# Two-layer mixer encoder, 512 x 1024, on one core: six places of the written order of ScalarE and VectorE and the place of the gates' bias rows

## The chip, the core and the metric

The kernel runs on one core of a Trainium2 chip. A core has five engines that work side by side: TensorE (PE, matrix products into the PSUM banks), VectorE (DVE), ScalarE (ACT), GpSimd (POOL) and SyncE (SP). In this kernel SP and POOL only issue transfers. PEld in the profile is PE loading stationary operands. The metric is the device time of one execution in microseconds, as the median of several; less is better.

## The reference, cut to what matters

```python
for l in range(2):                       # x: 512 tokens x 1024 channels, float32
    x = x + 0.5 * swiglu(rms_norm(x, ...), ffn1_w_in[l], ffn1_w_out[l])
    x = x + mixer(rms_norm(x, ...), ...)
    x = x + 0.5 * swiglu(rms_norm(x, ...), ffn2_w_in[l], ffn2_w_out[l])
return rms_norm(x, final_norm)

def mixer(h, ...):
    z = h @ w_in                         # columns: q, k, v (512 each), uf (512), ga, gf (1024 each)
    y_na = neighbourhood_attention(q, k, v, rpb) @ w_na_out   # 8 heads of 64
    y_f = fourier_mix(uf) @ w_f_out      # real part of a 2-D DFT per group of 128 channels
    g_na = sigmoid(ga + gate_bias[0])
    g_f = sigmoid(gf + gate_bias[1])
    return (g_na * y_na + g_f * y_f) @ w_o
```

A token attends to a window of 8 rows by 16 columns of its 8 x 64 grid, with a learned bias per head.

## The kernel before, in words

**Precision and splits.** Products are done in float32r: each operand is split into a high half (a copy that ACT rounds, `S.activation(hi, t, AF.Copy)`) and a low half (DVE, `t - hi`), and three products are summed (high by high, high by low, low by high; `mm3`, lines 293 to 295, and `late_low`, 469 to 472). So each new operand costs ACT one copy and DVE one subtraction before PE can use it. Weights are split in the same way: a `Stream` takes them in one fixed list, eight are fetched ahead into `raw` tiles (line 147), and `prep` makes `whi` on ACT (line 178) and `wlo` on DVE (line 181). There are three buffers each for `whi` and `wlo`. `ws.prep(ws.pos + n)` prepares weights until n are ready beyond the position of PE; `ws.next(ahead)` takes one and prepares `ahead` more.

**Seven products.** Products of two by two blocks (u with v, the gates, the output) take seven products of sums (Strassen's scheme), named m1 to m7, with combined activations t4 to t7 (`combos`) and three pairs of PSUM banks A, B, C that are snapshot (`snap`, line 539) or subtracted (`less`, line 544).

**The mixer's first part** (`proj_UV` and the block behind it): u and v together in seven parts, with the projections q0, k0, q1, k1 of the first head pairs between them (`proj_T`: 24 matmuls of 512 columns, 8 of the channel tiles by 3). Then come k's and q's of the other pairs, the DFT (`four_pos`, `rotated`, `four_ch`, `four_q`, `four_y`, `four_high`), the scores of head pairs 0 and 1 (`att_scores`, line 1212), their softmax (`Probs`: `maxes` on DVE, `exps` on ACT, `inverse` on DVE, `scaled` on ACT, line 1245), the transposes of the probabilities (line 1264) and the products with v (`att_pv`). v has four blocks of 128 rows, each with `v_high` on ACT (line 1046) and `v_low` on DVE (line 1049). `vs` are three more blocks, shifted by half a block: six copies from one part of the local memory to another, issued by SP (lines 1486 and 1487).

**What sets the order.** In this part the order of ACT, DVE and PE is written by hand (`tc.manual_schedule`): each engine runs its instructions in the order of the program text. The transfers are not in that list; they are placed by the scheduler and run in order on SP and POOL. Tiles come from pools with a fixed number of buffers: 23 of 4 KB per partition under the tag `k` (`slot`, `hilo`; weights, splits, snapshots and bias rows share them), 11 `tmp`, four `bm` (attention bias), 8 PSUM banks. An instruction whose tile takes over a buffer waits for that buffer's last reader.

**The gates** follow: rows of n (`fill(o, ns, 0, w)`: the attention's output times its matrix), then two gate blocks in the order m1, m5, m2, m6, m7, m3, m4, whose weights are partly sums made by accumulating transfers on POOL (lines 149 and 183). Two bias rows of 1024 (`gb`, line 1606) are fetched to all partitions and read at line 1350.

Of the kernel before, what the change touches and what calls it, by code (L numbers as in the profile page):

```python
# [9 lines left out]
F32 = mybir.dt.float32  # L10
F32R = mybir.dt.float32r
# [6 lines left out]
P = 128  # L18
# [71 lines left out]
def encoder_kernel(  # L90
# [19 lines left out]
    def slot(dt=F32, s="k", shape=(4, 256)):  # L110
        return kp.tile([P, *shape], dt, tag="k", name=nm(s), bufs=23)
# [864 lines left out]
    def stage_mixer(l, norm, nxt):  # L976
# [25 lines left out]
        def proj_T(scale, ahead=AHEAD, hook=None):  # L1002
            ps = bank()
            wh, wl = ws.next(ahead)
            for kt in range(DT):
                if hook and kt == 5:
                    hook()
                c = slice(kt * P, (kt + 1) * P)
                mm3(ps, wh[:, c], wl[:, c], *xs[kt], kt == 0, kt == DT - 1)

            def out():
                t = tmp(s="q")
                V.tensor_tensor(t, ps, R, ALU.mult)
                hi, lo = hilo("q")
                if scale is None:
                    S.activation(hi, t, AF.Copy)
                else:
                    S.activation(hi, t, AF.Copy, scale=scale)

                def rest():  # L1020
                    if scale is None:
                        V.tensor_tensor(lo, t, hi.bitcast(F32), ALU.subtract)
                    else:
                        V.scalar_tensor_tensor(lo, t, scale, hi.bitcast(F32), ALU.mult, ALU.subtract)
                    return hi, lo

                return rest

            return out

        def high_of(t, s):

            hi, lo = hilo(s)
            S.activation(hi, t, AF.Copy)

            def low_of():
                V.tensor_tensor(lo, t, hi.bitcast(F32), ALU.subtract)
                return hi, lo

            return low_of  # L1040
# [3 lines left out]
        def v_high(b, src):  # L1044
            vt[b] = slot(F32R, "v", (2, T))
            S.activation(vt[b][:, 0, :], src, AF.Copy, scale=norm.r[:, b : b + 1])

        def v_low(b, src):
            V.scalar_tensor_tensor(
                vt[b][:, 1, :], src, norm.r[:, b : b + 1], vt[b][:, 0, :].bitcast(F32), ALU.mult, ALU.subtract  # L1050
            )

        def proj_UV():

            acts, combine = combos(norm, None)
            ws.depth = 8
            steps = {m: combine(m) for m in (5, 6, 7, 4)}

# [12 lines left out]
            next(root)  # L1071
            ws.items[ws.prepped + 1].summed()
            next(root)
            norm.spread(R)
            ws.prep(ws.pos + 3)
            low10 = norm.quad_high(*norm.due.pop(0))
            s1 = snap(pa)
            norm.low01()
            step(6, 2)
            pb = pair("B")  # L1080
            product(pb, acts[5], K4, True, hook=low10)
            sb = snap(pb)
            S.activation(small("sq", 1), ones, AF.Exp)
            step(6)
            q0 = proj_T(DH**-0.5)
            step(7, 2)
            product(pa, acts[6], K4, False, again=True, hook=lambda: step(7))
            s2 = snap(pa)
            k0 = proj_T(None)
            step(4, 2)  # L1090
            q0 = q0()
            step(4)
            pc = pair("C")
            product(pc, acts[2], K4, True)
# [24 lines left out]


            k1 = proj_T(None, hook=turn)
            constants()
            us, ue = [[], []], []
            for c in range(2):
                for op in (ALU.add, ALU.subtract):
                    w = tmp(s="ue")
                    V.scalar_tensor_tensor(w, s1[:, c, :], norm.r[:, c : c + 1], flipped[c], ALU.mult, op)
                    ue.append(high_of(w, "u"))
                    us[c].append(None)
            for i, low_of in enumerate(ue):  # L1130
# [315 lines left out]
        with tc.manual_schedule(engines={mybir.EngineType.DVE, mybir.EngineType.Activation}):  # L1446
            with tc.manual_schedule(engines={mybir.EngineType.PE}):
# [7 lines left out]
                bt.append(rotated(fp[1]))  # L1455
                bh.append(high_of(bt[1], "b"))
                less(pa, sb)
                for c in range(2):
                    v_high(2 + c, sb[:, c, :])
                k[1] = k1()  # L1460
                b_ = [bh[0](), bh[1]()]
                q2 = proj_T(DH**-0.5)
# [1 line left out]
                p0, p1 = [Probs(i, att_scores(i)) for i in range(2)]  # L1464
                p0.maxes(0)
                p0.maxes(1)
                p0.exps(0)
                p1.maxes(0)
                p0.inverse(0)
# [2 lines left out]
                p0.inverse(1)  # L1472
                p1.exps(0)
                product(pa, acts4, K4, False, again=True, ahead=0)
                ws.prep(ws.pos + 1)
                q[2] = q2()
                for c in range(2):
                    v_high(c, pa[c])
                f0, f1 = four_ch(b_[0]), four_ch(b_[1])
                g0, g1 = four_q(f0[1]), four_q(f1[1])  # L1480
                for c in range(4):
                    v_low(c, sb[:, c - 2, :] if c > 1 else pa[c])
                vs = []
                for s in range(3):
                    t = slot(F32R, "vs", (2, T))
                    nc.sync.dma_start(out=t[0:64].bitcast(F32), in_=vt[s][64:128].bitcast(F32))
                    nc.sync.dma_start(out=t[64:128].bitcast(F32), in_=vt[s + 1][0:64].bitcast(F32))
                    vs.append(t)
                bias_for(1)
                p1.exps(1)  # L1490
                fp = [four_pos(2), four_pos(3)]
# [1 line left out]
                p1.inverse(0)  # L1493
                y1 = four_y(f1[0], g1)
                p1.inverse(1)
                ws.prep(ws.pos + 2)
                k2 = proj_T(None, 1)
                y0 = four_high(y0)
                y1 = four_high(y1)
                p0.scaled(0)  # L1500
                p0.scaled(1)
                bt = [rotated(fp[0])]
                bh = [high_of(bt[0], "b")]
                p1.scaled(0)
                bt.append(rotated(fp[1]))
                bh.append(high_of(bt[1], "b"))
                p1.scaled(1)
                b_ = [bh[0](), bh[1]()]
                k2 = k2()
                ws.prep(ws.pos + 2)  # L1510
                fq = []

                def second():
# [4 lines left out]
                g0, g1 = four_q(f0[1]), four_q(f1[1])  # L1518
                w0 = four_y(f0[0], g0)
                w1 = four_y(f1[0], g1)  # L1520
                w0 = four_high(w0)
                w1 = four_high(w1)
                yf += [y0(), y1()]
                q3 = q3()
                ts = transposed(p0.s) + transposed(p1.s)
                ph = [high_of(t, "p") for t in ts]
                ph = [h() for h in ph]
                pt_ = {0: ph[0:2], 1: ph[2:4]}
                p2, p3 = [Probs(i, att_scores(i)) for i in (2, 3)]
# [69 lines left out]
        att_outs(3)  # L1599
        t12, _ = next(first)  # L1600
        ws.prep(ws.pos + 2)
        bias = []
        for which in range(2):
            b_ = slot(F32, "gb", (D,))
            src = bass.AP(tensor=gbias.tensor, offset=gbias.offset + (2 * l + which) * D, ap=[[0, P], [1, D]])
            nc.sync.dma_start(out=b_, in_=src)
            bias.append(b_)
        acts = {1: (hx[0], lx[0], 0), 2: (hx[1], lx[1], 0), 3: (hx[1], lx[1], 256), 4: (hx[0], lx[0], 256)}

        def high(src, s):  # L1610
# [20 lines left out]
            w = [ws.next(), ws.next()]  # L1631
        for _ in fill(o, ns, 0, w):
            pass

        def behind_weights():
            return tc.issue_after(ws.items[ws.prepped - 1].last.ins)
# [253 lines left out]
```

## Time and profile before

| | us |
|---|---|
| median of 3 runs | 1923.67 (1921.34 to 1924.65) |
| the profiled execution, its device time | 1926.9 |
| its span, first to last instruction | 1923.7 |
| PE busy / DVE / ACT / POOL | 1894.6 / 1639.2 / 1193.4 / 171.5 |
| granted clock of PE, mean | 0.995 |

The span has six stages: FFN, mixer, FFN, and the same again. Times in the text are from the span's start. The first layer's mixer begins near 335 us and its gates near 500; the second layer's mixer begins near 1290.

How to read a line of the timeline: start, duration, engine, line of the code, operation, written tile <- read tiles, shapes, count; in brackets, how long the engine stood idle before it, and what ended that. `x2` means that two instructions in a row are put together. A matmul line has the time to the end of its result, while the next one starts earlier: a 512-column matmul shows 0.39 us and starts every 0.227 us at full clock.

### The profile page before, as it was taken

How to read it: one execution, taken by the hardware profiler on the slowest of the kernel's cores; microseconds unless marked ns; L12 is line 12 of the kernel's file. 1: busy time of each engine (PE TensorE's matmuls, PEld its weight loads, DVE VectorE, ACT ScalarE, POOL GpSimd, SP SyncE). 2: the span in 40 equal slices, each digit the busy share in tenths (PEclk: the TensorE clock that was granted, in tenths of full speed). 3: DMA queues.
4: the chain of work that ended last, by engine and by line, in shares of the span. 5: the costliest groups of instructions: out<-in, count | busy, mean ns of one | idle time of the engine just before them, and what ended most of it. 6: DMA issues, size and time to landing. Idle time of an engine off the chain costs nothing.

```text
span 1923.7 us, 25086 instructions
## 1 busy us (share of the span) xinstructions
PE 1894.6 (98%) x9149; PEld 1583.0 (82%) x9149; DVE 1639.2 (85%) x1992; ACT 1193.4 (62%) x1714; POOL 171.5 (9%) x210
## 2 busy tenths in 40 slices
PE   9999999999999999999999999999999999999998
PEld 7888888887788888888888888888788878888886
DVE  8878899776889987789998878998769889777899
ACT  6655666658555855566665556666685567555664
POOL 0100010100111010101010100101001101010010
PEclk9999999999999999999999999999999999999999
DMA  9776498931986777749877765988229867776594
GB/s 298 204 212 176 153 257 262 215 98 50 258 200 174 168 202 208 185 149 256 254 178 218 183 175 168 273 261 179 83 91 264 214 159 173 210 182 176 169 274 142
DMA packets 106939, 372.74 MB, mean 194 GB/s; under 512 B 12288, under 2 KB 12416, under 8 KB 106816
## 3 DMA queue, kind: packets, MB, share of 16 engines
q1 hardware_dynamic: 78144, 272.80, 42.2%
q0 software_dynamic: 28528, 98.33, 28.2%
q8 instruction: 71, 1.16, 0.2%
q14 instruction: 52, 0.43, 0.1%
q10 hardware_dynamic: 144, 0.02, 0.0%
HBM read 365.85 MB, written 2.11 MB: 191 GB/s over the span
## 4 chain that ended last, share of the span: by engine, by line
PE 80%; DVE 7%; DMA 5%; issue 4%; ACT 4%; POOL 0%; SPq 0%; DVEq 0%; ACTq 0%; POOLq 0%
PE A L469 9%; PE A L470 9%; PE A L472 9%; PE o L472 6%; PE o L470 6%; PE o L469 5%; PE B L469 5%; PE B L470 5%; PE B L472 5%; DMA raw<-in_wst_dram 4%; PE C L470 2%; PE C L469 2%; PE C L472 2%; DVE wlo L181 2%; PE ps L295 2%
## 5 line engine op out<-in xcount | busy, mean ns | idle before, releaser
L181 DVE TENSOR_TENSOR wlo<-raw,whi 128x1024 fp32r<-128x1024 f32 (+1 forms) x536 | 638.0, 1197 | 185.5 <-ACT whi L178 184.4
L178 ACT ACTIVATE whi<-raw 128x1024 fp32r<-128x1024 f32 (+1 forms) x536 | 553.1, 1037 | 387.7 <-PE A L470 127.8
L149 POOL DMA_DIRECT2D raw<-in_wst_dram x166 | 144.4, 896 | 1412.8 <-DMA raw<-in_wst_dram 740.8
L163 DVE TENSOR_TENSOR raw<-raw,raw 128x1024 f32<-128x1024 f32 (+1 forms) x150 | 178.1, 1196 | 1.2
L470 PE MATMUL A<-whi,xl 128*128 128x512 f32 x400 | 155.7, 389 | 0.0
L469 PE MATMUL A<-whi,xh 128*128 128x512 f32 x400 | 155.7, 389 | 0.0
L472 PE MATMUL A<-wlo,xh 128*128 128x512 f32 x400 | 115.1, 389 | 0.0
L174 DVE SCALAR_TENSOR_TENSOR wlo<-raw,whi 128x1024 fp32r<-128x1024 f32 (+1 forms) x83 | 98.1, 1198 | 15.8 <-ACT whi L173 15.8
L173 ACT ACTIVATE whi<-raw 128x1024 fp32r<-128x1024 f32 (+1 forms) x83 | 85.8, 1036 | 40.6 <-PE o L470 12.8
L674 ACT ACTIVATE th<-sn,rh 128x512 f32<-128x512 f32 x80 | 56.8, 714 | 70.7 <-DVE sn L544 70.7
L539 ACT ACTIVATE sn<-A 128x512 f32<-128x512 f32 x104 | 60.7, 589 | 46.5 <-PE A L472 46.3
L472 PEld LDWEIGHTS A<-wlo,xh 128*128 128x128 f32 x400 | 74.9, 188 | 15.8 <-DVE wlo L174 0.3
L470 PEld LDWEIGHTS A<-whi,xl 128*128 128x128 f32 x400 | 75.1, 188 | 15.4
L469 PEld LDWEIGHTS A<-whi,xh 128*128 128x128 f32 x400 | 75.1, 188 | 15.4
L469 PE MATMUL C<-whi,xh 128*128 128x512 f32 x208 | 81.1, 390 | 0.0
L470 PE MATMUL C<-whi,xl 128*128 128x512 f32 x208 | 81.0, 389 | 0.0
L470 PE MATMUL B<-whi,xl 128*128 128x512 f32 x208 | 81.0, 389 | 0.0
L469 PE MATMUL B<-whi,xh 128*128 128x512 f32 x208 | 80.9, 389 | 0.0
L472 PE MATMUL C<-wlo,xh 128*128 128x512 f32 x208 | 59.8, 389 | 0.0
L472 PE MATMUL B<-wlo,xh 128*128 128x512 f32 x208 | 59.8, 389 | 0.0
L293 PE MATMUL ps<-xh,whi 128*128 128x512 f32 x128 | 52.3, 409 | 4.3 <-ACT fq L1168 2.5
L469 PE MATMUL B<-whi,t5h 128*128 128x512 f32 x136 | 54.2, 399 | 0.0
(447 smaller groups left out, 4798.7 us busy)
## 6 DMA issues: line engine op xcount, KB each, us to landing
raw<-in_wst_dram SPq DMA_DIRECT2D x470, 512.0 KB, 5.3
raw<-in_wst_dram POOLq DMA_DIRECT2D x174, 512.0 KB, 8.0
raw<-in_wst_dram SPq DMA_DIRECT2D x30, 256.0 KB, 4.2
bm<-in_bias_dram SPq DMA_DIRECT2D x16, 384.0 KB, 3.7
vs<-v SPq DMA_DIRECT2D x12, 256.0 KB, 4.6
x<-in_xin_dram SPq DMA_DIRECT2D x4, 512.0 KB, 10.2
raw<-in_wst_dram POOLq DMA_DIRECT2D x8, 256.0 KB, 9.1
dft<-in_dft_dram POOLq DMA_DIRECT2D x8, 256.0 KB, 4.2
```

Of the source, the lines that this page charges most:

```text
L149: G.dma_start(out=self.t, in_=wst[GRAN_AT[self.plus]][:, 0 : self.n], accum_op=ALU.add)
L163: V.tensor_tensor(self.raw.t, self.raw.t, self.add.t, ALU.add)
L173: S.activation(hi, t, AF.Copy, scale=-1.0)
L174: self.last = V.scalar_tensor_tensor(lo, t, -1.0, hi.bitcast(F32), ALU.mult, ALU.subtract)
L178: S.activation(hi[:, cs], t[:, cs], AF.Copy)
L181: self.last = V.tensor_tensor(lo[:, cs], t[:, cs], hi[:, cs].bitcast(F32), ALU.subtract)
L293: PE.matmul(ps, lh, rh, start=start, stop=False, skip_group_check=again)
L469: PE.matmul(ps, lh, rh, start=start, stop=False, skip_group_check=again)
L470: PE.matmul(ps, ll, rh, start=False, stop=False, skip_group_check=again)
L472: PE.matmul(ps, lh, rl, start=False, stop=stop, skip_group_check=again)
L539: S.activation(t[:, b, :], ps[b], AF.Copy)
L674: S.activation(th[:, b, :], g[:, b, :], AF.Tanh, scale=norm.rh[:, c : c + 1])
```

## The change

Six places of the written order are changed, and the bias rows' fetch. No instruction is added or left out, and no PE order changes.

1. In `proj_UV`, t7 is made in three steps at three places instead of two: the subtraction behind q0's product, the high half in the hook of m6's product, the low half behind k0's product.
2. The high halves of v's rows 2 and 3 go from behind `less(pa, sb)` to behind k2's product; the weight of k2 is prepared ahead of p0's exponentials instead of behind m4's product.
3. The low halves of v's rows 2 and 3, and the copies `vs`, go behind the preparation of k3's weight.
4. q3's weight is prepared behind the first `rotated` (after the high halves of y), not ahead of k2's product.
5. `scaled` of p0 and p1 and the high halves of b are interleaved in another order.
6. q3's evacuation is cut in two: t (DVE) ahead of the high halves of w and the low halves of y, the high half (ACT) behind the high halves of the transposed probabilities.
7. The two bias rows are fetched behind the rows of n.

```diff
-            def out():
+            def out(now=True):
...
-                if scale is None:
-                    S.activation(hi, t, AF.Copy)
-                else:
-                    S.activation(hi, t, AF.Copy, scale=scale)
+                def high():
+                    if scale is None:
+                        S.activation(hi, t, AF.Copy)
+                    else:
+                        S.activation(hi, t, AF.Copy, scale=scale)
+                    return rest
...
-                return rest
+                return high() if now else high
...
             q0 = proj_T(DH**-0.5)
-            step(7, 2)
+            step(7)
             product(pa, acts[6], K4, False, again=True, hook=lambda: step(7))
             s2 = snap(pa)
             k0 = proj_T(None)
+            step(7)
             step(4, 2)
...
                 less(pa, sb)
-                for c in range(2):
-                    v_high(2 + c, sb[:, c, :])
                 k[1] = k1()
...
                 p0.maxes(0)
                 p0.maxes(1)
+                ws.prep(ws.pos + 3)
                 p0.exps(0)
...
                 product(pa, acts4, K4, False, again=True, ahead=0)
-                ws.prep(ws.pos + 1)
                 q[2] = q2()
...
-                for c in range(4):
-                    v_low(c, sb[:, c - 2, :] if c > 1 else pa[c])
-                vs = []
...
+                for c in range(2):
+                    v_low(c, pa[c])
                 bias_for(1)
...
                 p1.inverse(1)
-                ws.prep(ws.pos + 2)
-                k2 = proj_T(None, 1)
+                k2 = proj_T(None, 0)
+                for c in range(2):
+                    v_high(2 + c, sb[:, c, :])
                 y0 = four_high(y0)
                 y1 = four_high(y1)
+                bt = [rotated(fp[0])]
+                ws.prep(ws.pos + 1)
                 p0.scaled(0)
+                bh = [high_of(bt[0], "b")]
                 p0.scaled(1)
-                bt = [rotated(fp[0])]
-                bh = [high_of(bt[0], "b")]
-                p1.scaled(0)
                 bt.append(rotated(fp[1]))
                 bh.append(high_of(bt[1], "b"))
+                p1.scaled(0)
                 p1.scaled(1)
                 b_ = [bh[0](), bh[1]()]
                 k2 = k2()
                 ws.prep(ws.pos + 2)
+                for c in range(2):
+                    v_low(2 + c, sb[:, c, :])
+                vs = []
...
                 fq = []
...
                 w1 = four_y(f1[0], g1)
+                q3 = q3(False)
                 w0 = four_high(w0)
                 w1 = four_high(w1)
                 yf += [y0(), y1()]
-                q3 = q3()
                 ts = transposed(p0.s) + transposed(p1.s)
                 ph = [high_of(t, "p") for t in ts]
+                q3 = q3()
                 ph = [h() for h in ph]
...
         ws.prep(ws.pos + 2)
-        bias = []
-        for which in range(2):
-            b_ = slot(F32, "gb", (D,))
...
         for _ in fill(o, ns, 0, w):
             pass
+        bias = []
+        for which in range(2):
+            b_ = slot(F32, "gb", (D,))
...
```

More of the change, by code (lines that the diff above doesn't have):

```diff
@@ L1480, in stage_mixer @@
                 g0, g1 = four_q(f0[1]), four_q(f1[1])
-                for c in range(4):
-                    v_low(c, sb[:, c - 2, :] if c > 1 else pa[c])
-                vs = []
[L1484 to L1488, printed above, removed]
+                for c in range(2):
+                    v_low(c, pa[c])
                 bias_for(1)
@@ L1510, in stage_mixer @@
                 ws.prep(ws.pos + 2)
+                for c in range(2):
+                    v_low(2 + c, sb[:, c, :])
+                vs = []
+                for s in range(3):
+                    t = slot(F32R, "vs", (2, T))
+                    nc.sync.dma_start(out=t[0:64].bitcast(F32), in_=vt[s][64:128].bitcast(F32))
+                    nc.sync.dma_start(out=t[64:128].bitcast(F32), in_=vt[s + 1][0:64].bitcast(F32))
+                    vs.append(t)
                 fq = []
@@ L1601, in stage_mixer @@
         ws.prep(ws.pos + 2)
-        bias = []
-        for which in range(2):
-            b_ = slot(F32, "gb", (D,))
-            src = bass.AP(tensor=gbias.tensor, offset=gbias.offset + (2 * l + which) * D, ap=[[0, P], [1, D]])
-            nc.sync.dma_start(out=b_, in_=src)
-            bias.append(b_)
         acts = {1: (hx[0], lx[0], 0), 2: (hx[1], lx[1], 0), 3: (hx[1], lx[1], 256), 4: (hx[0], lx[0], 256)}
@@ L1633, in stage_mixer @@
             pass
+        bias = []
+        for which in range(2):
+            b_ = slot(F32, "gb", (D,))
+            src = bass.AP(tensor=gbias.tensor, offset=gbias.offset + (2 * l + which) * D, ap=[[0, P], [1, D]])
+            nc.sync.dma_start(out=b_, in_=src)
+            bias.append(b_)
         def behind_weights():
```

## The prediction

> **What bounds the kernel now.** I read the page first: TensorE (PE) is busy for all but 29 us of the span, so a changed order can win only idle PE time and time at a lowered clock.
>
> ```profile
> span 1923.7 us, 25086 instructions
> PE 1894.6 (98%) x9149; PEld 1583.0 (82%) x9149; DVE 1639.2 (85%) x1992; ACT 1193.4 (62%) x1714; POOL 171.5 (9%) x210
> ```
>
> Then PE's waits between 320 and 480 us, which is the first layer's mixer up to its attention (the columns: total, times, longest):
>
> ```profile
> PE ps L293 <- ACT fq L1168: 1.3, 1, 1.3
> PE ps L1212 <- DVE q L1013: 1.2, 1, 1.2
> PE ps L294 <- DVE b L1037: 1.1, 1, 1.1
> PE ps L293 <- DVE p L1037: 1.0, 1, 1.0
> ```
>
> All are waits for ACT or DVE; the second layer has the same four. So in this stretch the two engines' common chain, not PE, sets the end, while the stretches behind it have almost no PE idle (windows; first the length, then PE busy, later DVE busy):
>
> ```profile
> 404.20:437.60 33.40, 28.77 (x173) 24.15 (x170) 24.89 (x64) 23.07 (x50) 0.00 (x0) 0.99 0.33 88
> 416.50:421.50 5.00, 5.00 (x23) 4.13 (x22) 5.00 (x13) 3.17 (x9) 0.00 (x0) 1.00 0.66 158
> 455.00:484.00 29.00, 29.00 (x184) 25.43 (x183) 16.99 (x55) 25.60 (x73) 0.00 (x0) 1.00 0.16 55
> 560.00:1280.00 720.00, 719.88 (x3465) 605.07 (x3464) 629.69 (x670) 442.41 (x571) 66.25 (x78) 1.00 0.74 203
> ```
>
> So whatever PE gains by 455 us stays. From 404.2 to 437.6 DVE is busy for 24.89 of 33.40 us: 8.5 us idle. DVE's rows show the ends of that stretch (end of the b lows, first maximum of p2) and the waits:
>
> ```profile
> 402.91 1.29 DVE L1037 TENSOR_TENSOR b<-bt,b 128x512 fp32r<-128x512 f32 x2
> ...
> 406.96 1.23 DVE L181 TENSOR_TENSOR wlo<-raw,whi 128x1024 fp32r<-128x1024 f32 x1 [2.76 <-ACT whi L178]
> ...
> 414.51 1.23 DVE L181 TENSOR_TENSOR wlo<-raw,whi 128x1024 fp32r<-128x1024 f32 x1 [1.77 <-ACT whi L178]
> ...
> 429.34 1.23 DVE L181 TENSOR_TENSOR wlo<-raw,whi 128x1024 fp32r<-128x1024 f32 x1 [1.65 <-ACT whi L178]
> ...
> 435.20 2.48 DVE L1037 TENSOR_TENSOR p<-ps,p 128x512 fp32r<-128x512 f32 x4 [1.18 <-ACT p L1034]
> ...
> 437.60 0.42 DVE L1228 CUSTOM_DVE_ANT_0 s<-ps,bm 128x256 f32<-128x256 f32 x1
> ```
>
> ACT's rows show where the first two come from:
>
> ```profile
> 404.64 1.34 ACT L1046 ACTIVATE v<-sn,r 128x512 fp32r<-128x512 f32 x2 [2.72 <-PE ps L1212]
> ...
> 409.94 0.63 ACT L1018 ACTIVATE q<-q 128x512 fp32r<-128x512 f32 x1 [3.01 <-PE A L470]
> ...
> 414.38 1.24 ACT L1046 ACTIVATE v<-A,r 128x512 fp32r<-128x512 f32 x2
> 415.52 0.63 ACT L1168 ACTIVATE fq<-ps 128x255 f32<-128x255 f32 x2
> ...
> 419.82 1.36 ACT L1182 ACTIVATE y<-fy 128x512 fp32r<-128x512 f32 x2 [1.73 <-DVE fy L1175]
> ```
>
> The high halves of v's rows 2 and 3 need only `sb`, yet they wait 2.72 us for the first scores: their buffers are, I take it, those of q0 and k0, which these scores read last. Behind them stand m4's second weight and then q2's high half, which waits another 3.01 us for a product that it doesn't read: a full buffer pool again.
>
> **The change, part by part.** No arithmetic is added. The same DVE instructions lie between the b lows and p2's first maximum, so p2 moves by what becomes of the 8.5 us idle.
>
> *v's high halves 2 and 3 go behind k2's product, k2's weight ahead of p0's exponentials.* ACT is free at 404.64 - 2.72 = 401.9, makes m4's weight by 403, and DVE its low half at 404.2: the wait of 2.76 goes. q2's product then gives t at 405.4 and its high half at 406.1 to 406.7, now in q0's buffer, released at 404.6. k2's weight follows to 407.7 while DVE does p0's maxima until 407.4: a wait of 0.35 in place of 1.77. Next late are v's highs 0 and 1: ACT ends its three exponential pairs at 410.5 (2.9 us, as between the high half of 409.94 and the weight that DVE splits at 414.51) and PE its product at about 410.2, so DVE waits 0.3 near 411.2. The reads of pa and fq now end by 412.6, so k2's product finds its bank at 414.5: the PE wait of 1.3 goes.
>
> *q3's weight and the order of rotated and scaled.* From 410.5 ACT does two v highs (1.24), two fq (0.63), an exponential pair (about 1), two more v highs (1.34), two y highs (1.36), and then q3's weight (1.04), ready at 417. DVE ends its first rotated at 416.1 and waits 0.85: a new wait, with the second rotated and both b lows queued behind it. They end at 421.6 instead of 427.0; PE asks for b at 423.4 (414.5, plus 39 matmuls at 5.00/22 = 0.227 us, from the window row). The 1.1 goes. The scaled of p0 and p1 end near 422.4, ahead of the transposes at 427.
>
> *v's low halves 2 and 3 behind k3's weight.* The wait for that weight's high half stays, 1.65 plus 0.15 for ACT's scaled ahead of it. The two lows stood ahead of the b lows; they now stand ahead of the w rows: neutral on DVE. The moved weight steps issue no loads: eight weights are fetched ahead, and this stage's are out by then. POOL's queue is not touched.
>
> *q3's t ahead of the y lows, its high half behind the p highs.* The bank is free at 428.7, before PE asks, and ACT can start the p highs earlier: the waits of 1.18 (DVE) and 1.2 and 1.0 (PE) go.
>
> Left of DVE's idle: 0.35 + 0.3 + 0.85 + 0.15 + 1.8 = 3.4 us. So p2's maxima come 8.5 - 3.4 = **5.1 us** earlier. From there to p3's scaled the order is unchanged, and the chain arrives 5.1 us earlier there too. PE gets there sooner still: k3 at 430.7, 24 matmuls to 436.1, 36 shorter and longer ones to about 442, and the first eight transposes to 443. Its last transposes wait for p3's scaled:
>
> ```profile
> 449.72 1.71 ACT L1245 ACTIVATE s<-s,rs 128x256 f32<-128x256 f32 x4
> ...
> 451.08 0.87 PE L1264 MATMUL ps<-ident,s 128*128 128x128 f32 x6 [0.36 <-ACT s L1245]
> ```
>
> ACT is there at 444.6 now, so the hole of 0.8 us (0.4 and 0.4) becomes one of about 3 (2.4 and 0.6). That is the new bound of the stretch, and the gain is the chain's 5.1, not PE's 6. The second layer also has a wait of 0.45 of its own now, which put its maxima 0.3 later; its gain is 5.4:
>
> ```profile
> 1384.93 0.42 DVE L1173 TENSOR_TENSOR fy<-ps,fq 128x256 f32<-128x256 f32 x1 [0.45 <-DVE fq L1167]
> ```
>
> *The hole and the clock.* Windows of 3.41 us at the borders where the granted clock changes (eighth number):
>
> ```profile
> 412.72:416.13 3.41, 2.13 (x18) 1.93 (x17) 1.64 (x3) 3.41 (x10) 0.00 (x0) 1.00 0.54 181
> 433.20:436.61 3.41, 1.54 (x14) 1.28 (x15) 2.23 (x5) 2.55 (x6) 0.00 (x0) 1.00 0.00 0
> 436.61:440.02 3.41, 3.41 (x10) 2.65 (x9) 3.41 (x11) 2.92 (x10) 0.00 (x0) 0.50 0.02 5
> 525.36:528.77 3.41, 3.41 (x9) 2.65 (x8) 3.41 (x3) 1.90 (x2) 0.56 (x1) 0.50 1.02 303
> 1385.52:1388.93 3.41, 1.99 (x26) 1.64 (x24) 2.75 (x7) 1.89 (x4) 0.00 (x0) 1.00 0.01 2
> ```
>
> A window in which PE was busy for 1.54 or 1.99 us is followed by half clock, one with 2.13 isn't. Three idle microseconds within 3.3 leave at least one window under 2.0 however the borders fall. Half a window, **1.7 us**, is lost behind the hole, in the part that PE bounds. (Today's two slow stretches lie ahead of the chain's end and cost nothing.) If the second window is caught too it is 3.4; bounds 0 and 3.4. The Trainium skill's page "TensorE: Matmul & The Clock Gate", section "Why this matters for your kernels", speaks against this loss: it asks for no idle gap above some 3 us, one idle window bringing half clock. By that rule no clock would be lost; the rows here show half clock behind windows that were 45 and 58% busy.
>
> *t7 in three places, around k0.* ACT made t7's high half, waiting for DVE, ahead of k0's weight. Now the weight goes first, and a PE wait of 0.5 goes:
>
> ```profile
> 360.93 0.50 PE L295 MATMUL ps<-xh,wlo 128*128 128x512 f32 x1 [0.48 <-DVE wlo L181]
> ```
>
> t7's product starts some 28 us later; its lateness is hidden. If that cover were gone, the cost would be one split, 1.2 us.
>
> *The copies `vs` on SP.* Four of the six now follow the v lows that end at 426.5.
>
> ```profile
> 417.08 0.53 SPq L1486 DMA_DIRECT2D vs<-v  x1
> ...
> 420.83 1.10 SPq L1487 DMA_DIRECT2D vs<-v  x1
> ...
> 440.91 1.08 SPq L1197 DMA_DIRECT2D bm<-in_bias_dram  x2
> ...
> DMA to landing us min/median/max: 3.1/4.6/5.2
> ```
>
> Six issues take 4.85 us now; four from 426 land by 434.5 at the latest, and the first product that reads one starts at 436.1. Hidden, with some 2 us to spare.
>
> *The bias rows on SP.* They are issued behind c's first weight instead of ahead of it:
>
> ```profile
> 484.30 1.01 SPq L1606 DMA_DIRECT2D gb<-in_gbias_dram x2
> ...
> 516.56 0.75 DVE L1350 SCALAR_TENSOR_TENSOR sn<-sn,r,gb 128x512 f32<-128x512 f32 x1
> ...
> 522.77 1.06 ACT L178 ACTIVATE whi<-raw 128x1024 fp32r<-128x1024 f32 x1 [2.43 <-DMA raw<-in_wst_dram]
> ...
> 524.36 0.50 PE L469 MATMUL A<-whi,t3h 128*128 128x512 f32 x1 [1.94 <-ACT sn L539]
> ...
> DMA to landing us min/median/max: 9.1/10.8/12.3
> ...
> PE A L469 <- ACT sn L539: 0.8, 1, 0.8
> ```
>
> Their first reader runs 32 us after the issue, and they land within 12.3 (the bias rows' own view): a few microseconds later is free. The last row is the same place in the second layer. The PE wait of 1.94 here hangs on an accumulated weight that starts only after its tile was split; I take no change, between 0 and the whole wait.
>
> Sum: first layer 5.1 + 0.5 - 1.7 = 3.9, second 5.4 + 0.5 - 1.7 = 4.2: **8.1 us**. The profiled execution took 1926.9, its span 1923.7; the median of the runs is 1923.67, and I take the 8.1 from that: **1915.6**.
>
> **Rivals.** *The clock holds*: the hole costs no window; 3.4 more, 1912.2. For it: two windows with the wait at 414 passed. Against: three idle microseconds are more than any of them had. It is what the Trainium skill's rule above would give.
>
> *The gates' hole closes*: without the bias rows ahead, the accumulated weights come early enough; 1.94, its slow window (525.36) of 1.7 and the second layer's 0.8 go: 4.4 more, 1911.2. Against: that weight waits for a DVE split, not for the queue.
>
> *The buffer pool stays full* (the change doesn't do what it says): q2's high half still waits until 409.9. Then k2's low half starts at 411.3, DVE waits 3.6 us more, and 5.1 shrinks to 1.6, which the clock eats: 1.3 left, 1922.4. For it: the pool's order is not in the profile.
>
> *Slower: the copies come too late.* If SP gives them out behind the next pair's bias rows (440.91, 435.3 after), the last is issued at 441.2 and lands at 446.4. PE needs it from 436 on; half of that product, the rows of f and the transposes then end at 452.4, against 451.95 now, and the hole of 10 us costs at least a slow window, 1.7: 2.2 per layer, 1928. It decides once a copy lands some 10 us after its place in the sum.
>
> **How the numbers follow.** Forecast 0.45, clock holds 0.13, gates' hole closes 0.12, pool stays full 0.18, copies too late 0.12. This kernel's measurement can tell about 0.2%, 3.85 us, from no change: the first three are faster (0.70), the fourth the same (0.18), the fifth slower (0.12). The range reaches from both faster rivals nearly together, 1908, to the pool's case, 1923; beyond it lie the copies.
>
> **What would show it.** Right: ACT's q2 row no longer waits for A; no PE waits for fq, b or q3; p2's maxima 5 us sooner; a PE wait of 2 to 3 us at L1264 for s, with a half-clock window behind it. Wrong: q2 still waiting near 410 for PE; PE waiting at L293 to L295 for vs; L1350 waiting for gb.

## The result and the profile after

The changed kernel takes **1907.09 us** (median of 4 runs, 1904.92 to 1907.68), the kernel before 1923.45 (4 runs beside it, 1921.34 to 1924.65): a ratio of 0.9914, 95% interval 0.9897 to 0.9931, or 16.4 us less. The prediction said 8.1 less, and at the lowest 1908. So the direction was right and the size wrong by half.

The section on the change says that no PE order changes. That holds for the order written by hand. Outside it the program's scheduler also moved something when the bias rows were moved: two neighbouring products in the rows of n changed places on PE, and on ACT the high half of t1 came forward. The second of these gave a late transfer 1.2 us more room, as the experiments show.

The page and PE's waits over the whole span, after:

```profile
span 1902.9 us, 25094 instructions
PE 1885.3 (99%) x9149; PEld 1580.2 (83%) x9149; DVE 1639.2 (86%) x1992; ACT 1194.7 (63%) x1714; POOL 171.5 (9%) x210
```

```profile
PE ps L1269 <- ACT s L1250: 4.8, 4, 2.0
...
PE A L469 <- ACT sn L539: 0.4, 1, 0.4
```

The waits for fq, b, q, p and for k0's weight are gone, and the hole for p3's scaled has come where the prediction put it (line 1264 before is line 1269 now). But the gates' wait (A for sn) has shrunk from 2.8 us to 0.4, which the prediction had left standing.

To see where the time came from, one reads the start of the same matmul in both traces. These are, twice (once for each layer), the first matmul of k0, of m2's product C behind it, of the rows of n, and of the gates' product B. Before:

```profile
359.84 0.39 PE L293 MATMUL ps<-xh,whi 128*128 128x512 f32 x1
366.09 0.39 PE L469 MATMUL C<-whi,xh 128*128 128x512 f32 x1
487.66 0.39 PE L293 MATMUL ps<-whi,o 128*128 128x512 f32 x1
530.20 0.39 PE L469 MATMUL B<-whi,xh 128*128 128x512 f32 x1
...
1313.79 0.39 PE L293 MATMUL ps<-xh,whi 128*128 128x512 f32 x1
1320.01 0.39 PE L469 MATMUL C<-whi,xh 128*128 128x512 f32 x1
1441.92 0.39 PE L293 MATMUL ps<-whi,o 128*128 128x512 f32 x1
1481.73 0.39 PE L469 MATMUL B<-whi,xh 128*128 128x512 f32 x1
```

After:

```profile
358.85 0.39 PE L293 MATMUL ps<-xh,whi 128*128 128x512 f32 x1
364.29 0.39 PE L469 MATMUL C<-whi,xh 128*128 128x512 f32 x1
480.70 0.39 PE L293 MATMUL ps<-whi,o 128*128 128x512 f32 x1
519.43 0.39 PE L469 MATMUL B<-whi,xh 128*128 128x512 f32 x1
...
1302.88 0.39 PE L293 MATMUL ps<-xh,whi 128*128 128x512 f32 x1
1308.32 0.39 PE L469 MATMUL C<-whi,xh 128*128 128x512 f32 x1
1424.14 0.39 PE L293 MATMUL ps<-whi,o 128*128 128x512 f32 x1
1463.46 0.39 PE L469 MATMUL B<-whi,xh 128*128 128x512 f32 x1
```

The differences between neighbouring rows give the length of each stretch:

| stretch | layer 1: before, after, gain | layer 2: before, after, gain | forecast gain |
|---|---|---|---|
| k0 | 6.25, 5.44, **0.81** | 6.22, 5.44, **0.78** | 0.5 + 0.5 |
| mixer and attention | 121.57, 116.41, **5.16** | 121.91, 115.82, **6.09** | 3.4 + 3.7 |
| gates | 42.54, 38.73, **3.81** | 39.81, 39.32, **0.49** | 0 |

That is 17.1 us. The two profiled spans differ by 20.8; the other 3.7 us lie where the change touches nothing (0.99 of it ahead of k0: 359.84 against 358.85). Such stretches vary from execution to execution; the execution profiled before was 3.2 above its median, the one after 2.2 below.

In the gates' first layer, 1.9 of the 3.81 is PE's wait, and most of the rest is the half-clock window that stood behind it (525.36 in the prediction). The window doesn't always come: in e1, a kernel described below, the second layer has a wait of 1.95 and the window and takes 42.55, the first has a wait of 1.57 and no window and takes 40.53.

In the mixer's chain, the same rows as the prediction showed, after:

```profile
401.11 1.28 DVE L1041 TENSOR_TENSOR b<-bt,b 128x512 fp32r<-128x512 f32 x2
...
404.23 0.63 ACT L1021 ACTIVATE q<-q 128x512 fp32r<-128x512 f32 x1 [3.16 <-DVE q L1014]
...
405.84 1.22 DVE L181 TENSOR_TENSOR wlo<-raw,whi 128x1024 fp32r<-128x1024 f32 x1 [0.34 <-ACT whi L178]
...
421.73 1.23 DVE L181 TENSOR_TENSOR wlo<-raw,whi 128x1024 fp32r<-128x1024 f32 x1 [1.78 <-ACT whi L178]
...
430.06 0.42 DVE L1233 CUSTOM_DVE_ANT_0 s<-ps,bm 128x256 f32<-128x256 f32 x1
```

ACT's q2 no longer waits for PE's A but for DVE's own q. From b's low halves to p2's first maximum DVE takes 28.95 us (430.06 - 401.11), where it took 34.69 (437.60 - 402.91): 5.74 less. In the second layer it is 6.07 less (28.96 against 35.03). The prediction had 5.1 and 5.4.

The hole and what ran behind it, first layer and second. First the windows of the granted clock (eighth number), then PE's rows:

```profile
440.37:443.78 3.41, 1.03 (x8) 0.56 (x7) 2.49 (x4) 2.76 (x7) 0.00 (x0) 1.00 0.47 156
443.78:447.19 3.41, 3.41 (x28) 3.08 (x28) 2.29 (x6) 2.43 (x7) 0.00 (x0) 0.50 0.00 0
1382.44:1385.86 3.42, 2.31 (x15) 1.79 (x13) 3.33 (x7) 1.58 (x4) 0.00 (x0) 1.00 0.15 35
1385.86:1389.27 3.41, 2.14 (x20) 1.62 (x20) 1.83 (x4) 3.36 (x8) 0.00 (x0) 1.00 0.30 119
```

```profile
442.74 0.44 PE L1269 MATMUL ps<-ident,s 128*128 128x128 f32 x2 [2.02 <-ACT s L1250]
443.54 1.35 PE L1269 MATMUL ps<-ident,s 128*128 128x128 f32 x6 [0.36 <-ACT s L1250]
444.82 2.74 PE L1217 MATMUL ps<-q,q 64*128 64x256 f32 x24
447.49 0.50 PE L293 MATMUL ps<-whi,y 128*128 128x512 f32 x1
...
1386.77 0.44 PE L1269 MATMUL ps<-ident,s 128*128 128x128 f32 x2 [2.01 <-ACT s L1250]
1387.56 0.88 PE L1269 MATMUL ps<-ident,s 128*128 128x128 f32 x6 [0.36 <-ACT s L1250]
1388.37 1.32 PE L1217 MATMUL ps<-q,q 64*128 64x256 f32 x13
1389.91 0.97 PE L1217 MATMUL ps<-q,q 64*128 64x256 f32 x11 [0.21 <-DVE p L1041]
1390.91 0.50 PE L293 MATMUL ps<-whi,y 128*128 128x512 f32 x1
```

The two holes are alike (2.02 and 2.01, then 0.36). In the first layer one window holds nearly all of it, PE is busy for 1.03 us in it, and half clock follows. In the second the border of two windows cuts the hole, 2.31 and 2.14 are left, and the clock holds. From the hole's end to the rows of y the first layer takes 4.75 us and the second 4.14: the half-clock window cost 0.6, not 1.7. The second layer's 4.14 holds a wait of 0.21 for p that the first doesn't have, so by estimate the slower matmuls alone cost some 0.8.

### The profile page after: what moved, and what is told of

Its sections match the earlier page's. It is cut to its first block, busy times and chain, and to the rows that moved or that the text cites. A ratio compares the mean times of both kernels' runs of the same rounds, so it can differ in the third digit from the quotient of the medians.

```text
span 1902.9 us, 25094 instructions
## 1 busy us (share of the span) xinstructions
PE 1885.3 (99%) x9149; PEld 1580.2 (83%) x9149; DVE 1639.2 (86%) x1992; ACT 1194.7 (63%) x1714; POOL 171.5 (9%) x210
## 4 chain that ended last, share of the span: by engine, by line
PE 89%; DVE 5%; ACT 3%; issue 2%; DMA 1%; DVEq 0%; POOL 0%; ACTq 0%; POOLq 0%
PE A L469 10%; PE A L470 10%; PE A L472 10%; PE o L470 7%; PE o L469 7%; PE o L472 7%; PE B L469 5%; PE B L470 5%; PE B L472 5%; PE C L469 2%; PE C L470 2%; PE C L472 2%; PE tr L592 2%; PE ps L293 2%; PE ps L294 2%; PE ps L295 2%
## 5 line engine op out<-in xcount | busy, mean ns | idle before, releaser
L694 DVE TENSOR_TENSOR at<-at,at 128x1024 f32<-128x1024 f32 (+1 forms) x48 | 53.8, 1130 | 0.0
```

The costliest lines, as they stand in the source:

```text
L694: V.tensor_tensor(dst, in0, in1, op)
```

## The experiments

Theories at the start. **A**: the bias rows' move closed the gates' hole. **C** (the prediction's): the rows' place is worth nothing. For the mixer: the prediction's reasons, place by place, with their sizes open. Twelve runs follow, one of them the changed kernel again (e9), in three groups; the kernel before, run beside each group, had medians of 1923.01, 1922.59 and 1922.97.

### The gates

**e1**, the changed kernel with the rows' fetch back at its old place; **e2**, the kernel before with the rows' move alone:

```diff
         ws.prep(ws.pos + 2)
+        bias = []
+        for which in range(2):
...
+            bias.append(b_)
         acts = {1: (hx[0], lx[0], 0), 2: (hx[1], lx[1], 0), 3: (hx[1], lx[1], 256), 4: (hx[0], lx[0], 256)}
...
         for _ in fill(o, ns, 0, w):
             pass
-        bias = []
-        for which in range(2):
...
-            bias.append(b_)
```

(This is e1; e2 makes the opposite move in the kernel before.)

> The changed kernel with the bias rows' fetch alone at its old place, ahead of the rows of n; all else as changed. On SP the two issues stand ahead of three weight loads again, and on ACT the high half of t1 stands again behind the four splits of o instead of ahead of them. Theory A (the bias rows' move closed the gates' hole, 3.8 us in the first layer and 0.4 in the second): 1911.3, 4.2 above the changed kernel, with PE's wait of about 2 us at the gates' last product of A back in the first layer. Theory C (the prediction: the rows' place is worth nothing; the hole closed because the mixer delivers earlier): 1907.1, no such wait.

> The kernel before with the bias rows' move alone. Theory A: the gates' hole closes here too: 4.2 to 4.4 us off, 1919.2, and PE does not wait for ACT's sn at the gates. Theory C: 1923.4, and the wait of 1.9 us stays, since the mixer is as late as before.

e1: 1909.0 (ratio to before 0.9929, 0.9915 to 0.9942), 1.9 above the changed kernel, with gate waits of 1.6 and 1.9 us in its profile (of an execution of 1912.4). e2: 1919.75 (0.9985, 0.9976 to 0.9994), 3.3 below before, with waits of 0.2 and 0.5. e1's interval overlaps the changed kernel's, so its 1.9 isn't certain by itself; e2's lies below 1. So C falls by e2: moving the rows is worth some 3 us by itself, 1.2 to 4.6 by the interval.

**e3** asks in which way. The rows stay late, t1's high half is tied behind the last split of o:

```diff
-            S.activation(hi, src, AF.Copy)
+            split.last = S.activation(hi, src, AF.Copy)
...
-            h1 = high(t12, "t1")
+            with tc.issue_after(split.last.ins):
+                h1 = high(t12, "t1")
```

> The changed kernel with the bias rows at their new place, but the high half of t1 on ACT tied behind the last split of o, where it stood before the change. It parts two ways in which the rows' move can act. Theory A1 (order: t1's high half goes ahead on ACT, so m1's weight and all of DVE's work at the gates run 1.2 us earlier): PE waits again for some 0.7 to 2 us in the first layer, and with its half-clock window the time is 1909 to 1911. Theory A2 (transfer: two rows read by all partitions stand ahead of the weights on the queue, and the weights land later): nothing changes, 1907.1.

1907.92 (1906.78 to 1913.3; ratio 0.9927, 0.9912 to 0.9941): by the median, between the two theories and nearer to A2. But three runs lie at 1906.8 to 1907.9 and two at 1912.4 and 1913.3, and the profile is of the 1912.4. The tie also let some of ACT's snapshots and weights at the gates change their order, so t1 isn't all that e3 moves. The traces say more. In the timeline of before, ACT, DVE and POOL at the gates, and the weight that PE waits for:

```profile
491.03 1.06 ACT L1612 ACTIVATE t1h<-t 128x1024 fp32r<-128x1024 f32 x1
492.00 1.04 ACT L173 ACTIVATE whi<-raw 128x1024 fp32r<-128x1024 f32 x1
493.07 1.22 DVE L174 SCALAR_TENSOR_TENSOR wlo<-raw,whi 128x1024 fp32r<-128x1024 f32 x1 [1.61 <-ACT whi L173]
...
514.80 0.85 POOL L183 DMA_DIRECT2D raw<-in_wst_dram  x1 [11.72 <-DVE wlo L181]
```

After:

```profile
480.16 1.06 ACT L1614 ACTIVATE t1h<-t 128x1024 fp32r<-128x1024 f32 x1 [0.33 <-DVE t L1594]
...
484.26 1.21 DVE L174 SCALAR_TENSOR_TENSOR wlo<-raw,whi 128x1024 fp32r<-128x1024 f32 x1
...
506.55 0.85 POOL L183 DMA_DIRECT2D raw<-in_wst_dram  x1 [15.58 <-DVE wlo L181]
...
513.62 1.06 ACT L178 ACTIVATE whi<-raw 128x1024 fp32r<-128x1024 f32 x1 [0.31 <-PE A L470]
```

And e3, first and second layer:

```profile
509.11 0.86 POOL L183 DMA_DIRECT2D raw<-in_wst_dram  x1 [15.30 <-DVE wlo L181]
...
514.99 1.06 ACT L178 ACTIVATE whi<-raw 128x1024 fp32r<-128x1024 f32 x1 [0.32 <-PE A L470]
...
1453.58 0.85 POOL L183 DMA_DIRECT2D raw<-in_wst_dram  x1 [16.41 <-DVE wlo L181]
...
1461.76 1.06 ACT L178 ACTIVATE whi<-raw 128x1024 fp32r<-128x1024 f32 x1 [2.66 <-DMA raw<-in_wst_dram]
```

Before, t1's high half comes on ACT behind the splits of o, m1's weight behind it, and DVE waits 1.61 us; everything that DVE does at the gates hangs on that, up to the split which releases the accumulation of line 183. After, t1 is ahead of three of the splits and DVE doesn't wait. Against the first matmul of t2's product, the accumulation is issued 1.9 us early in the kernels with t1 forward (1.88 to 1.93 in all 20 stretches of ten traces) and 0.7 early in those with t1 late (0.65 to 0.69 in 8 of 8, e3 among them). PE needs the sum about 5.2 us after that matmul. In e3's first layer ACT split the sum 5.9 us after the issue (509.11 to 514.99; it waited last for PE, not for the transfer, and PE then didn't wait), in the second 8.2 after it (1453.58 to 1461.76: PE waits 2.2). So two things are shown: the order of t1 gives the transfer 1.2 us more room, and the landing varies by over 2 us, so that a single execution may show a wait of 2 us or none.

The landing times in all fourteen traces bear this out. The transfer landed 5.5 to 8.1 us after its issue, and PE's wait is what goes beyond 5.9 us where t1 is late (8 stretches; 7.86 and a wait of 1.94 in the first layer of before) and beyond 7.1 where it is forward (20 stretches; 7.56 and 0.42 in the second layer of after), to within 0.1 us. By estimate, the 28 landings together give a mean wait of 1.05 us a layer with the smaller room and 0.25 with the larger. A half-clock window, some 1.7 us, followed in three of the 8 late stretches and in none of the 20. Over two layers that makes about 2.9 us for the order alone, near e2's 3.3. That the rows' own bytes also delay the transfer isn't excluded, but not shown: with the rows in front it landed after 6.7 to 7.9 us (six stretches, mean 7.4), with them behind after 5.5 to 8.1 (22 stretches, mean 6.8), and the difference is smaller than the spread.

### The mixer, place by place

**e4**, v's high halves 2 and 3 back behind `less(pa, sb)`:

```diff
                 less(pa, sb)
+                for c in range(2):
+                    v_high(2 + c, sb[:, c, :])
...
                 k2 = proj_T(None, 0)
-                for c in range(2):
-                    v_high(2 + c, sb[:, c, :])
```

> The changed kernel with the high halves of v's rows 2 and 3 back at their old place on ACT, ahead of k1's. The prediction's reason (they wait for buffers that the first scores read last, and m4's weight and DVE stand behind them): DVE's wait of some 2.7 us for m4's weight returns, k2's and the b rows' later waits swallow some of it, so p2's maxima come 2 to 2.5 us later in each layer: 1911 to 1912. Rival (they are ready when ACT comes to them and cost only their own 1.3 us on ACT, which has idle time there): under 1 us in all, 1907 to 1908.

1914.14 (0.9952, 0.9940 to 0.9965): 7.0 above the changed kernel, more than expected. ACT in its trace:

```profile
403.49 1.34 ACT L1050 ACTIVATE v<-sn,r 128x512 fp32r<-128x512 f32 x2 [2.73 <-PE ps L1217]
...
408.78 0.63 ACT L1021 ACTIVATE q<-q 128x512 fp32r<-128x512 f32 x1 [3.01 <-PE A L470]
```

Both waits of the kernel before are back, the one for the scores (2.73) and, behind it, q2's for a product that it doesn't read (3.01): the buffers, as the prediction took them, explain both, and this one place moves p2's maxima by 3.5 us in each layer. The 2 to 2.5 expected had left out the second wait.

**e5**, t7 in three places alone, in the kernel before:

```diff
-            step(7, 2)
+            step(7)
...
             k0 = proj_T(None)
+            step(7)
```

> The kernel before with the three-place t7 alone. The prediction's term: PE's wait of 0.48 at k0 goes, 0.5 a layer, 1922.4. Theory now (a short stall costs PE more than the idle time shown, since the next matmuls start late as well: 0.87, 0.34 and 0.24 between starts where 0.227 is usual): 0.8 a layer, 1921.8, and in the trace the first matmul of C after k0 starts 0.8 earlier against the one of t6's product. Rival (t7's later halves hold up its own product): no gain, a new PE wait at t7's product near 387.

1920.88 (0.9993, 0.9984 to 1.0002): not certain by the time, but by the trace: the stretch of k0 is 5.44 us long in both layers, as in the changed kernel, against 6.25 and 6.22. A wait of 0.48 cost 0.8.

**e6**, q3's evacuation whole, behind the y lows:

```diff
-                q3 = q3(False)
...
                 yf += [y0(), y1()]
+                q3 = q3()
...
-                q3 = q3()
```

> The changed kernel with q3's evacuation as before: t, high half and all behind the y lows. The prediction's reason (ACT's high half stands ahead of the p highs, DVE's p lows wait 1.2 for them, and PE waits for q's bank and for p): p2's maxima come about 1.2 us later in each layer, 2.4 in all, 1909.5, with PE's waits at the scores for q and at k3 for p back. Rival (with the chain now earlier, PE is as far behind that the two waits are hidden): under 0.5 a layer, 1907 to 1908.

1910.6 (0.9937, 0.9923 to 0.9950): 3.5 above. DVE waits 1.24 us for p again and PE 0.96 at k3 for p, while the wait at the scores for q did not return; p2's maxima come 1.3 later in each layer. That makes 2.7 of the 3.5. The rest is not explained: the two kernels' intervals overlap, and the profile has a wait of 1.6 us for x behind the mixer, where nothing was changed.

**e10**, q3's weight and the order of rotated, scaled and b as before:

```diff
-                k2 = proj_T(None, 0)
+                ws.prep(ws.pos + 2)
+                k2 = proj_T(None, 1)
...
+                p0.scaled(0)
+                p0.scaled(1)
                 bt = [rotated(fp[0])]
-                ws.prep(ws.pos + 1)
-                p0.scaled(0)
                 bh = [high_of(bt[0], "b")]
-                p0.scaled(1)
+                p1.scaled(0)
...
-                p1.scaled(0)
                 p1.scaled(1)
```

> The changed kernel with q3's weight and the order of rotated, scaled and b's high halves as before (q3's weight ahead of k2's product). The other parts undone singly cost 7.0 (v's high halves), 3.5 (q3), 1.7 (t7) and 1.9 to 3.3 (bias rows) of 16.4, so if the parts add up, 1 to 2 us are left for this place: 1908 to 1909. The prediction's reason (b's low halves come 1 to 2 us later and PE waits for b again): a PE wait at L294 for b, near 420. Rival (this order is worth nothing once v's high halves are away): 1907.1, no wait for b.

1905.43 (0.9909, 0.9896 to 0.9922), no wait for b, p2's maxima 0.4 *earlier* in each layer. The rival held: with v's halves away, this part of the change is no gain and costs a little. The intervals don't tell that from nothing, but the chain shows it in both layers: DVE's wait of 0.34 for q3's weight isn't there in e10.

**e9**, the changed kernel again, as the measure for e10 to e12:

> The changed kernel again, as the measure for the three runs beside it and for the spread of the gates' wait: 1907.1 by its four runs so far. By theory A1 the wait for the accumulated weight is the landing time (5.9 to 8.2 us in the profiles so far) less 7.1 us, so 0 to 1.1 us a layer; a profile with a landing under 7.1 shows no wait, one over it shows the difference.

1907.51 (0.9918, 0.9906 to 0.9930). In the second layer the transfer landed after 7.8 us, with a wait of 0.6. In this execution the same holes of 2.0 us were followed by half clock in both layers, and its stretches from C to the rows of n are 116.56 and 116.62 long.

### The hole

**e7** moves p3's inverses and scaled ahead of the low halves of k2 and q3; **e8** also k3's low half ahead of the split of o:

```diff
                 p3.exps(0)
+                p3.inverse(0)
                 ws.prep(ws.pos + 2)
                 p3.exps(1)
+                p3.inverse(1)
+                p3.scaled(0)
+                p3.scaled(1)
                 k[2] = k2()
...
+                k[3] = k3()        # e8
                 att_split(0, po[0])
-                p3.scaled(0)
-                p3.scaled(1)
```

> A step on: the changed kernel with p3's inverses and scaled moved up, ahead of the low halves of k2 and q3 and ahead of k3's evacuation. The hole that the forecast named (PE waits 2.0 and 0.4 us in each layer for p3's scaled) should go; next late is k3's low half, which the scores of the next pair read, about 1.0 us after PE's new arrival: 1.4 a layer off, 1904.3. Rival (the hole is passed on whole to the next wait, since ACT does as much work before it): within 0.5 us of 1907.1, with PE waiting as long at L1217 for q as it did for s.

> As the run before, and k3's low half also ahead of the split of o. If k3's low half is what is late next, PE finds it in time and the hole goes nearly whole: 2.2 to 2.9 a layer, 1901.3 to 1902.7, without the half-clock window behind it. If the splits of o or the p halves are late next instead: as the run before, 1904.3, with PE's wait at another operation.

1906.88 (0.9920, 0.9906 to 0.9933) and 1908.61 (0.9927, 0.9914 to 0.9940): nothing gained, twice. PE's new wait in e7:

```profile
PE ps L1217 <- DVE o L300: 2.7, 2, 1.3
```

The hole moved to the next scores, which take over the bank of po: not k3's low half but the split of o was late next (in e8 1.9 us, since that split came later still). And in e7 PE did get to the rows of y 1.3 us sooner in the first layer, only for half clock to fall on them:

```profile
442.83:446.24 3.41, 2.03 (x23) 1.66 (x23) 3.17 (x8) 1.87 (x5) 0.00 (x0) 1.00 0.12 49
446.24:449.65 3.41, 3.41 (x12) 2.57 (x9) 3.35 (x14) 3.41 (x11) 0.00 (x0) 0.50 0.00 0
```

From C to the rows of n, e7 takes 116.57 in the first layer and 115.09 in the second, where the clock held: there the window cost 1.5.

**e11** puts k3's t behind p3's first inverse, k3's high half and one half of the first split of o between p3's two scaled, and the other half of that split behind them, all ahead of the transposes of p2 and p3; **e12** does the same with the second split of o. `att_split(0, po[0], (0,))` is the first half of the first split:

```diff
                 p3.exps(0)
+                p3.inverse(0)
+                k3 = k3(False)
                 ws.prep(ws.pos + 2)
                 p3.exps(1)
-                k[2] = k2()
-                q[3] = q3()
-                p3.inverse(0)
-                k3 = k3()
                 p3.inverse(1)
...
+                p3.scaled(0)
+                k[2] = k2()
+                att_split(0, po[0], (0,))
+                k3 = k3()
+                q[3] = q3()
+                att_split(1, po[1], (0,))   # e12
+                p3.scaled(1)
+                k[3] = k3()
+                att_split(0, po[0], (1,))
+                att_split(1, po[1], (1,))   # e12
...
-                att_split(0, po[0])
-                p3.scaled(0)
-                p3.scaled(1)
                 ts = transposed(p2.s) + transposed(p3.s)
-                k[3] = k3()
...
-                att_split(1, po[1])         # e12
```

> A step on from the two runs with p3's scaled moved up, in which PE then waited 1.3 to 1.9 us for the split of o (its bank): k3's t, its high half and the first split of o are put between p3's inverses and scaled, in ACT's and DVE's gaps before PE's last transposes. If the split of the first o was next late: PE's wait of 1.3 goes, one of about 0.4 to 1 for the second o's bank stays; 1 to 2 a layer, 1903 to 1905. If the hole is only passed on again: within 0.5 of the changed kernel.

> As the run before, and the second o's split too, ahead of the p halves. If the banks of both o were what the scores waited for, PE runs through: no wait over 0.4 us between 435 and 455, no half-clock window there, 2.5 to 3.3 a layer, 1900.5 to 1902. If the p halves or the next pair's maxima are late instead, the wait shows there, and the time is that of the run before.

1902.37 (0.9897, 0.9883 to 0.9911) and **1900.23** (1899.92 to 1900.36; 0.9880, 0.9867 to 0.9894). e11 keeps a wait of 1.1 us a layer for the second o's split, which e12 takes away. Of e12's PE waits over the whole span, the longest two behind the program's start:

```profile
PE A L469 <- ACT sn L539: 0.8, 1, 0.8
PE o L470 <- DVE c4l L300: 0.7, 1, 0.7
```

The first lies at the gates, the second in an FFN: from C to the rows of n no wait of 0.2 us or more is left, and the span has no half-clock window but at its end. That stretch takes 112.62 and 112.61 us, 4.0 less than in e9, where a half-clock window fell into it in both layers; that is somewhat more than was expected. This is the fastest of the kernels here, 7.3 under the changed kernel beside it, their intervals apart.

## Why the prediction was right or wrong

- **The mixer's chain: right, a little small.** 5.1 and 5.4 were said; 5.74 and 6.07 came. DVE's waits left are 0.34, 0.18, 0.34, 0.16 and 1.78, 2.8 in place of the 3.4 summed up. The step "DVE ends its first rotated at 416.1 and waits 0.85" was too dear: 0.34 came. The 8.5 also held two waits that the prediction doesn't name (0.74 and 0.14, ahead of p0's inverses); they went as well. By e4, e6 and e10 the chain's gain is 3.5 from v's high halves, 1.3 from q3 and -0.4 from b's order; some 1.3 is left for v's low halves, k2's weight ahead of p0's exponentials and the parts together, not tried alone.
- **The buffers: right.** The waits left with the place of v's high halves and came back with it in e4, so the rival of the full pool falls (in its sum, 5.1 - 3.6 is 1.5, not 1.6). That the buffers are q0's and k0's is still read from the scores' row, which ends the wait.
- **b's reason: wrong.** b's low halves that "end at 421.6 instead of 427.0" came about (6.0 us sooner against C), but not through the place they were put down to: in e10, without it, they come another 0.3 sooner, and PE doesn't wait for b either.
- **The hole: right in place and cause, 2.0 and 0.36 us for 2.4 and 0.6.**
- **The clock: the mechanism right, the size wrong, one of the two steps that carry the miss.** "Half a window, 1.7 us, is lost behind the hole, in the part that PE bounds": the window came, but over transposes and scores of 64 rows, where it cost 0.6 (in e7, over 512-column matmuls, 1.5). That no border could save it was said of three idle microseconds within 3.3; the hole had 2.4, and a border did save the second layer. That was luck, since in e9 both layers were caught. By the rule of the Trainium skill's page "TensorE: Matmul & The Clock Gate", section "Why this matters for your kernels", named in the prediction, no clock would have been lost to an idle gap of 2.0 us; the trace's first layer disagrees. The Trainium skill's page "TensorE: Matmul & The Clock Gate" also says, in Part 1 on the HAM clock gate, that the window runs freely and doesn't start anew with the kernel; with that the traces agree, since the same hole got half clock in one layer here and in both layers of e9. Both layers caught, the mixer's gain is 5.0 + 5.3 (121.57 - 116.56, 121.91 - 116.62), for 7.1 forecast.
- **k0: a term too small.** The idle time, 0.48, was counted; 0.8 came.
- **The bias rows: the step that failed, a term put at nothing.** "I take no change, between 0 and the whole wait" looked only at the rows' own lateness, and at the queue. Right was that the weight waits for a DVE split; wrong was that this split can't come sooner: with the fetch moved, t1 came forward on ACT, and the split with it by 1.2 us. The rival named the place, at 0.12 and 4.4 us, with another reason (the weights come earlier without the rows ahead); 3.81 + 0.49 came in the profile, 1.9 (e1) to 3.3 (e2) in the medians.
- **The copies on SP: right, free.** No PE wait names vs.

The stretches gained 17.1 in the profiles, for 8.1 forecast: 4.3 more at the gates, 2.8 more by the clock (0.6 lost of the 3.4 charged; with both layers caught, as in e9, some 1.5), 1.3 more by the chain and 0.6 more at k0. So the gates' nothing and the clock's size make most of the miss. Both faster rivals in full would be 1907.8; most of both came.

Together: 1.6 for k0, 10.3 to 11.3 for the mixers and 1.9 to 4.3 for the gates make 13.8 to 17.2; the interval of the ratio is 13.3 to 19.8. Open are the 1.3 a layer of the chain that no run tries alone, and whether the rows' own transfer has a share at the gates.

## What to carry to other kernels

Moving a transfer in a program whose order is partly made by a scheduler moves more than the transfer: compare the order of every engine first, and price what came forward. Behind a hole that closes, the next wait is the next reader of a bank or buffer, so list those in order (here scaled, the split of o, the second split) and move all, or nothing is gained, as in e7 and e8. A slow-clock window is priced by what runs in it, and a wait by the matmul starts it delays.

## What the hardware showed beyond that

- A short stall of PE costs more than its idle time. In before, the matmuls on both sides of k0's wait (that of 360.93 stands in the prediction):

```profile
360.07 0.39 PE L294 MATMUL ps<-xl,whi 128*128 128x512 f32 x1
...
361.27 0.40 PE L293 MATMUL ps<-xh,whi 128*128 128x512 f32 x1
361.51 0.40 PE L294 MATMUL ps<-xl,whi 128*128 128x512 f32 x1
```

  Starts are 0.86, 0.34 and 0.24 apart where 0.227 is usual. The stretch lost 0.81, 0.33 more than the 0.48 shown. Of that, 0.16 is how the idle time is counted (a row runs to the end of its result, 0.39, while the next could start after 0.227), and 0.11 is the late start of the next matmul.
- Half clock followed every window of 3.41 us with PE busy for 1.55 or less (22 of 22 between 100 and 1880 us in the fourteen traces), two of six between 1.69 and 2.03, none above 2.05.
- The same accumulating transfer of 512 KB landed 5.5 to 8.1 us after its issue (28 stretches in the fourteen traces); PE's wait behind it ran from none to 2.17 us with that.
